# A second stream of small mixers paced against large products: a later start of its turn and a lower rank

## The chip, the cores and the metric

The kernel runs on one core of a Trainium2 chip. The metric is the device time of one execution in microseconds (us). Five engines work side by side, each through its own queue in order: TensorE (PE, with the weight loads as PEld), VectorE (DVE), ScalarE (ACT), GpSimd (POOL) and SyncE (SP), which here only issues transfers.

## What is computed

One trunk layer of a hybrid backbone, for 256 prompt tokens and 2048 latent tokens on a 32 x 64 grid, all in fp32, model width 1024. With `u = h @ w_in` the layer is

```python
u_pool, u_hy, u_q, u_k, u_v = jnp.split(u, [s1, s2, s3, s4], axis=-1)
y_pool = pool_mixer(u_pool, pool_w, pool_scale)          # means over windows 2/4/8/16
y_hy = hyena_mixer(u_hy, ...)                            # two gated long convolutions by FFT
y_na = attend(q, k, v)                                   # q, k after QK-norm
x = x + gate1 * (jnp.concatenate([y_pool, y_hy, y_na], axis=-1) @ w_out)
h = rms_norm(x, norm2_g) * (1.0 + scale2) + shift2
x = x + gate2 * (jnp.square(jax.nn.relu(h @ w_up)) @ w_down)
```

The prompt attends to itself densely; a latent token attends to its grid neighbourhood and to 256 cached keys. The keys and values of the prompt are outputs too. Every large product is made of three fp32r products (high by high, high by low, low by high part), so each weight tile is split in two after it is loaded.

## The kernel before, in words

Three generators write the program; each `yield` gives an abstract cost. `weave` (L177) always takes the next step of the stream with the smallest ratio of cost so far to its weight, so the streams are written down interleaved.

- `dense`, weight 2200e3: first the products for `u` (five blocks of tokens: four of 512 latent tokens, one of 256 prompt tokens), then the q, k and v products (`qkv_run`, `proj_qkv`) for the blocks in the order 3, 4, 0, 1, 2, where 4 is the prompt. I call them qkv3, qkv4, qkv0, qkv1, qkv2. Each but the first begins by loading and normalising its tokens again (`xq`, L164 to L169). Then come output projection and MLP of the prompt and of the four latent bands.
- `latent_mixers`, weight 850e3: the filters of the latent convolutions, then `hyena` (a spectrum stage, an inverse stage, a second of each), then the latent attention, which is written after all q, k, v products and after the prompt's mixers.
- `prompt_mixers` (L856), weight 700e3: waits until qkv4 is written, then writes `prompt_filters` (small fp32 products `pb`), then `prompt_hyena` woven with `pooling` (both for all tokens' pooling and the prompt's convolutions), then the prompt's attention. Its two PSUM banks `b` and `bo` are its own.

The third number of a stream in L1271 is a rank offset. The instructions written in a step of that stream are ranked as if they had been written so many instructions earlier (`tc.high_priority`). When the program is built, a scheduler goes through a simulated run and gives each engine, among the instructions that are ready, the one of the lowest rank; that becomes the order of the engine's queue. The queues are then in order on the chip. Dense has offset 0, the latent mixers 1000, the prompt's mixers 2500.

As the prompt's stream has a ratio of zero when its wait ends, and its whole cost is less than what would bring its ratio level with the other streams, it is written in one piece between qkv4 and qkv0.

Of the kernel before, what the change touches and what calls it, by code (L numbers as in the profile page):

```python
# [55 lines left out]
def tile_hybrid_step(ctx: ExitStack, tc: tile.TileContext, a: dict):  # L56
# [115 lines left out]
    def at_rate(stream, f):  # L172

        for cost in stream:
            yield cost and cost * f

    def weave(*streams):  # L177


        live = [[st[0], float(st[1]), 0.0, st[2] if len(st) > 2 else 0] for st in streams]  # L180
        while live:
            for s in sorted(live, key=lambda e: e[2] / e[1]):
                try:
                    with tc.high_priority(s[3]) if s[3] else ExitStack():
                        cost = next(s[0])
                except StopIteration:
                    live.remove(s)
                    break
                if cost is not None:
                    s[2] += cost  # L190
                    yield cost
                    break
            else:
                yield None
# [10 lines left out]
    def wait_for(*names):  # L205
        while not done.issuperset(names):
            yield None

    def scope(name, bufs=2, side=None, **kw):
        return tc.tile_pool(name=name, bufs=bufs, side=side, reuse_waits="tile", **kw)  # L210
# [644 lines left out]

    def prompt_mixers():  # L856
        yield from wait_for("h2p", "qkv4", "ln")
        with scope("bps", 1, side="right", space=PSUM) as bps:
            def bank(tag="b"):
                return bps.tile([P, 512], F32, tag=tag, name="p" + tag)  # L860

            with scope("pfilt", side="right") as fp:
                yield from prompt_filters(fp, bank)
            with scope("phy", side="right") as fp:
                yield from weave((prompt_hyena(fp, bank), 14000), (pooling(fp, bank), 8100))
            with scope("pat", side="right") as at:
                for hp_ in range(4):
                    yield from attend_prompt(at, bank, hp_)
        done.add("prompt")
# [185 lines left out]
    def latent_mixers():  # L1055
        with scope("aps", 1, space=PSUM) as aps:
            turn = [0]

            def psum(tag=None):
                turn[0] ^= tag is None  # L1060
                return aps.tile([P, 512], F32, tag=tag or "fz"[turn[0]], name="pf")

            yield from filters(psum)
            done.add("filt")
            yield from wait_for("u")
            yield from wait_for("ln")
            with scope("hy") as kp:
                yield from at_rate(hyena(kp, psum), 0.55)
            done.add("hyena")
        yield from wait_for("qkv", "prompt")  # L1070
        with scope("att") as at, scope("attps", 2, space=PSUM) as aps:
            def bank(tag):
                return aps.tile([P, 512], F32, tag=tag, name="p" + tag, bufs={"s": 2, "pt": 2, "o": 1}[tag])

            mask = []
            for rc in range(3):
                for cc_ in range(3):
                    nr, ncol = ROWC[rc][1], COLC[cc_][1]
                    m = at.tile([P, nr, ncol], BF16, tag=f"mask{rc}{cc_}", name="mask", bufs=1)
                    nc.gpsimd.dma_start(out=m, in_=a["mask"][rc * 3 + cc_, :, 0:nr * ncol].rearrange("p (r c) -> p r c", c=ncol))  # L1080
                    mask.append(m)
            for band in range(4):
                yield from wait_for(*(f"qkv{b}" for b in range(max(band - 1, 0), min(band + 2, 4))))
                for hp_ in range(4):
                    yield from attend_latent(at, bank, mask, band, hp_)
                done.add(band)
        done.add("att")
# [180 lines left out]
                        yield from steps  # L1268
                        run = run2

    for cost in weave((dense(ctx.enter_context(ExitStack())), 2200e3), (latent_mixers(), 850e3, 1000), (prompt_mixers(), 700e3, 2500)):  # L1271
        assert cost is not None, "streams wait for each other"


# [175 lines left out]
def build(nc, arrays):  # L1450
    a = {}
    for name, v in arrays.items():
        a[name] = nc.dram_tensor(f"in_{name}", v.shape, mybir.dt.from_np(v.dtype), kind="ExternalInput").ap()
    for name, shape in _OUTS:
        a[name] = nc.dram_tensor(f"out_{name}", shape, F32, kind="ExternalOutput").ap()
    with tile.TileContext(nc, schedule_with_timeline_sim=True) as tc:
        tile_hybrid_step(tc, a)
# [18 lines left out]
```

## Time and profile before

| | us |
|---|---|
| median of 3 runs (lowest to highest) | 3167.44 (3164.95 to 3171.02) |
| the profiled execution | 3163.24 |
| its span, first to last instruction | 3161.5 |
| PE busy | 3022.6 (96%) |
| PEld busy | 2494.6 (79%) |
| DVE busy | 1936.3 (61%) |
| ACT busy | 1428.6 (45%) |
| POOL busy | 951.3 (30%) |

The profiled execution is the source of all rows. A busy PE is not PE at its peak: matmuls overlap and their ends are modelled. PEclk is the granted clock of TensorE as a share of full speed.

### The profile page before, as it was taken

How to read it: one execution, taken by the hardware profiler on the slowest of the kernel's cores; microseconds unless marked ns; L12 is line 12 of the kernel's file. 1: busy time of each engine (PE TensorE's matmuls, PEld its weight loads, DVE VectorE, ACT ScalarE, POOL GpSimd, SP SyncE). 2: the span in 40 equal slices, each digit the busy share in tenths (PEclk: the TensorE clock that was granted, in tenths of full speed). 3: DMA queues.
4: the chain of work that ended last, by engine and by line, in shares of the span. 5: the costliest groups of instructions: out<-in, count | busy, mean ns of one | idle time of the engine just before them, and what ended most of it. 6: DMA issues, size and time to landing. Idle time of an engine off the chain costs nothing.

```text
span 3161.5 us, 46164 instructions
## 1 busy us (share of the span) xinstructions
PE 3022.6 (96%) x16901; PEld 2494.6 (79%) x16901; DVE 1936.3 (61%) x3017; ACT 1428.6 (45%) x2721; POOL 951.3 (30%) x832
## 2 busy tenths in 40 slices
PE   5999998889998999999999999899999999999999
PEld 1667797788988988877878778688878888788887
DVE  7677676987568777876766655544564445634443
ACT  3555445545556666665555543323332333333222
POOL 2333233743243333454433321311231112311101
PEclk8999999999999999999999999999999999999999
DMA  6568667855875865733333325233324233232322
GB/s 222 160 215 298 220 217 244 277 167 169 269 231 184 297 197 161 230 117 107 123 113 119 106 91 189 80 100 107 107 89 152 93 100 114 88 125 94 100 94 87
DMA packets 255167, 494.26 MB, mean 156 GB/s; under 512 B 23763, under 2 KB 124824, under 8 KB 254619
## 3 DMA queue, kind: packets, MB, share of 16 engines
q1 hardware_dynamic: 247741, 469.03, 45.2%
q0 software_dynamic: 7200, 22.28, 2.5%
q8 instruction: 134, 2.20, 0.3%
q14 instruction: 92, 0.75, 0.1%
HBM read 421.86 MB, written 70.13 MB: 156 GB/s over the span
## 4 chain that ended last, share of the span: by engine, by line
PE 81%; DVE 8%; DMA 5%; issue 3%; ACT 2%; POOL 1%; SPq 1%; DVEq 0%; ACTq 0%; POOLq 0%
PE pm L126 22%; PE pm L127 22%; PE pm L128 22%; PE po L923 3%; PE ppt L902 2%; PE ps L888 1%; DVE wl L115 1%; PE ps L889 1%; PE pf L516 1%; PE pf L127 1%; DMA xq<-in_xT_sample 1%; PE pf L126 1%; PE pf L128 1%; PE pf L435 1%; DMA dftw<-in_S 1%
## 5 line engine op out<-in xcount | busy, mean ns | idle before, releaser
L115 DVE TENSOR_TENSOR wl<-wraw,wh 128x1024 fp32r<-128x1024 f32 x460 | 590.3, 1286 | 454.1 <-ACT wh L112 418.9
L112 ACT ACTIVATE wh<-wraw 128x1024 fp32r<-128x1024 f32 x430 | 454.5, 1058 | 781.8 <-PE pm L127 717.6
L126 PE MATMUL pm<-hh,wh 128*128 128x512 f32 (+1 forms) x1920 | 719.3, 377 | 22.7 <-ACT hh L112 12.8
L127 PE MATMUL pm<-hl,wh 128*128 128x512 f32 (+1 forms) x1920 | 718.1, 375 | 1.9 <-DVE hl L166 1.9
L128 PE MATMUL pm<-hh,wl 128*128 128x512 f32 (+1 forms) x1920 | 716.7, 374 | 0.0
L115 POOL TENSOR_TENSOR al<-r,ah 128x512 fp32r<-128x512 f32 (+1 forms) x160 | 200.5, 1255 | 964.6 <-ACT ah L112 959.3
L126 PE MATMUL pm<-ah,wh 128*128 128x512 f32 (+1 forms) x1280 | 473.9, 373 | 7.6 <-ACT r L1132 7.2
L128 PE MATMUL pm<-ah,wl 128*128 128x512 f32 (+1 forms) x1280 | 476.2, 373 | 0.0
L127 PE MATMUL pm<-al,wh 128*128 128x512 f32 (+1 forms) x1280 | 474.1, 371 | 0.0
L126 PEld LDWEIGHTS pm<-hh,wh 128*128 128x128 f32 x1920 | 365.9, 191 | 103.4 <-ACT hh L112 14.2
L127 PEld LDWEIGHTS pm<-hl,wh 128*128 128x128 f32 x1920 | 365.4, 190 | 74.1 <-issue 10.4
L128 PEld LDWEIGHTS pm<-hh,wl 128*128 128x128 f32 x1920 | 365.4, 190 | 69.0 <-issue 7.8
L1150 DVE SCALAR_TENSOR_TENSOR x<-pm,gate,x 128x512 f32<-128x512 f32 (+1 forms) x320 | 220.8, 695 | 286.0 <-PE pm L128 285.0
L126 PEld LDWEIGHTS pm<-ah,wh 128*128 128x128 f32 x1280 | 240.9, 188 | 51.5 <-ACT r L1132 7.4
L127 PEld LDWEIGHTS pm<-al,wh 128*128 128x128 f32 x1280 | 241.3, 189 | 43.1 <-issue 1.9
L128 PEld LDWEIGHTS pm<-ah,wl 128*128 128x128 f32 x1280 | 241.1, 188 | 43.1 <-issue 2.2
L127 PE MATMUL pm<-wl,hh 128*128 128x256 f32 x864 | 250.3, 292 | 5.7 <-DVE wl L115 5.7
L126 PE MATMUL pm<-wh,hh 128*128 128x256 f32 x864 | 248.9, 292 | 6.3 <-ACT hh L165 2.2
L128 PE MATMUL pm<-wh,hl 128*128 128x256 f32 x864 | 250.0, 293 | 2.1 <-POOL hl L115 2.1
L894 POOL TENSOR_SCALAR sS<-sS,rl 128x736 f32<-128x736 f32 (+5 forms) x128 | 125.0, 977 | 197.6 <-DVE rl L893 116.7
L127 PEld LDWEIGHTS pm<-wl,hh 128*128 128x128 f32 x864 | 169.0, 196 | 10.7 <-DVE wl L115 7.1
L126 PEld LDWEIGHTS pm<-wh,hh 128*128 128x128 f32 x864 | 168.0, 196 | 11.7 <-ACT hh L112 3.5
(325 smaller groups left out, 4784.3 us busy)
## 6 DMA issues: line engine op xcount, KB each, us to landing
wraw<-in_w_up SPq DMA_DIRECT2D x160, 512.0 KB
wraw<-in_w_down SPq DMA_DIRECT2D x160, 512.0 KB
wraw<-in_w_qkv SPq DMA_DIRECT2D x60, 512.0 KB
wraw<-in_w_u SPq DMA_DIRECT2D x40, 512.0 KB
dftw<-in_S POOLq DMA_DIRECT2D x40, 512.0 KB, 6.5
wraw<-in_w_out SPq DMA_DIRECT2D x40, 512.0 KB
x<-in_xT_sample SPq DMA_DIRECT2D x64, 256.0 KB
wm<-in_w_mod SPq DMA_DIRECT2D x64, 256.0 KB
```

Source lines behind the costliest of these rows:

```text
L112: nc.scalar.activation(hi, raw, AF.Copy)
L115: lo_eng.tensor_tensor(out=lo, in0=raw, in1=hi.bitcast(F32), op=ALU.subtract)
L126: nc.tensor.matmul(out, lh, rh, start=start, stop=False, **kw)
L127: nc.tensor.matmul(out, lh, rl, start=False, stop=False, **kw)
L128: nc.tensor.matmul(out, ll, rh, start=False, stop=stop, **kw)
L435: nc.tensor.matmul(pf[d][:, e * 256:(e + 1) * 256], lhs(r, e), f3n[r, o * 256:(o + 1) * 256], start=(e == 0), stop=True, skip_group_check= ...
L516: nc.tensor.matmul(pf, f3[r, o * 256 + c * P:o * 256 + (c + 1) * P], h2[r, b * 512:(b + 1) * 512], start=True, stop=True)
L888: nc.tensor.matmul(out, qh[:, qc], krhs, start=True, stop=False, **kw)
L894: nc.gpsimd.tensor_scalar(out=sc_[:, :tot], in0=sc_[:, :tot], scalar1=r, scalar2=1.0, op0=ALU.mult, op1=ALU.mult)
L902: nc.tensor.transpose(tr[:n, q * P:(q + 1) * P], scs[e][:, so:so + n], ident)
L923: nc.tensor.matmul(po[64 * e:64 * e + 64, ocol:ocol + P], vap(e, n), pt[:n, col * P:(col + 1) * P], start=(q == 0), stop=(q == len(chunks) ...
L1150: nc.vector.scalar_tensor_tensor(out=xs[j], in0=po, scalar=gate2[:, j, c:c + 1], in1=xs[j], op0=ALU.mult, op1=ALU.add)
```

## The change

The prompt's stream is charged 80e3 of cost as soon as its wait ends, before it writes anything, and its rank offset goes from 2500 to 1000. No operation is added or removed.

```diff
     def prompt_mixers():
         yield from wait_for("h2p", "qkv4", "ln")
+
+        yield 80e3
         with scope("bps", 1, side="right", space=PSUM) as bps:
...
-    for cost in weave((dense(ctx.enter_context(ExitStack())), 2200e3), (latent_mixers(), 850e3, 1000), (prompt_mixers(), 700e3, 2500)):
+    for cost in weave((dense(ctx.enter_context(ExitStack())), 2200e3), (latent_mixers(), 850e3, 1000), (prompt_mixers(), 700e3, 1000)):
```

## Rows read from the trace of the kernel before

**Rows 1.** Page, first lines: busy us, share of span, instructions.
```profile
PE 3022.6 (96%) x16901; PEld 2494.6 (79%) x16901; DVE 1936.3 (61%) x3017; ACT 1428.6 (45%) x2721; POOL 951.3 (30%) x832
```

**Rows 2.** Windows by engine: start:end, length, busy us and instructions, clock, DMA.
```profile
core 0: us, PE busy (x) PEld busy (x) DVE busy (x) ACT busy (x) POOL busy (x), PEclk, DMA share, GB/s
395.00:495.00 100.00, 99.36 (x685) 90.49 (x685) 68.42 (x82) 43.78 (x84) 32.63 (x27) 1.00 0.64 212
500.00:700.00 200.00, 171.45 (x1121) 149.37 (x1121) 173.71 (x250) 103.46 (x219) 123.11 (x119) 0.91 0.71 233
700.00:900.00 200.00, 186.47 (x1446) 175.79 (x1446) 117.91 (x166) 106.41 (x216) 62.89 (x59) 0.98 0.71 232
```

**Rows 3.** Windows of 50 us, same columns.
```profile
600.00:650.00 50.00, 39.71 (x214) 32.80 (x213) 48.45 (x68) 22.85 (x47) 37.72 (x37) 0.83 0.72 227
...
900.00:950.00 50.00, 50.00 (x424) 50.00 (x423) 41.75 (x60) 28.90 (x55) 19.73 (x15) 1.00 0.65 201
```

**Rows 4.** PE groups at 600:640, then at 680:720: count, busy, mean ns, idle before.
```profile
L126 PE MATMUL pm<-wh,hh 128*128 128x256 f32 x19 | 6.7, 365 | 0.2 <-ACT hh L112 0.2
...
L126 PE MATMUL pm<-wh,hh 128*128 128x256 f32 x92 | 25.7, 284 | 0.0
```

**Rows 5.** By tile: count, ns min/median/max, first and last start.
```profile
L719 SPq DMA_DIRECT2D h2p<-h2pd x1: 562/562/562, 393.4 to 393.4; - x1
...
L850 PE MATMUL pbo<-pS,pw x36: 377/379/796, 529.9 to 682.7; 128*128 128x256 f32 x36
...
L776 PE MATMUL pb<-zp,dpc x32: 377/379/620, 582.0 to 649.8; 128*128 128x256 f32 x32
L796 PEld LDWEIGHTS pb<-Yp,dpc x32: 186/190/338, 608.8 to 680.6; 128*128 128x128 f32 x32
L796 PE MATMUL pb<-Yp,dpc x32: 377/379/797, 608.9 to 680.8; 128*128 128x256 f32 x32
...
L966 SPq DMA_DIRECT2D yTp<-obp x4: 319/398/830, 728.3 to 814.8; - x4
L1104 SPq DMA_DIRECT2D yraw<-yTp x8: 327/332/1458, 875.6 to 979.3; - x8
```

**Rows 6.** DMA issues of SP in order of time: start, length, what is loaded or stored.
```profile
561.56 0.43 SPq L284 DMA_DIRECT2D out_new_kT<-qo  x1
...
605.70 0.82 SPq L1169 DMA_DIRECT2D xq<-in_xT_sample  x2
```

**Rows 7.** DVE groups at 500:700: count, busy us, mean ns, idle before.
```profile
L848 DVE SCALAR_TENSOR_TENSOR pS<-pS,kv,pE 128x256 f32<-128x256 f32 x18 | 13.0, 720 | 2.7 <-POOL pS L836 2.6
...
L847 DVE TENSOR_TENSOR pS<-pS,kv 128x8 f32<-128x8 f32 x4 | 0.6, 154 | 0.0
```

**Rows 8.** DVE groups, then PE groups, at 395:495, same columns.
```profile
L405 DVE RECIPROCAL rinv<-rinv 128x512 f32<-128x512 f32 x2 | 6.7, 3347 | 0.0
...
L747 DVE MEMSET Fp<- 1x256 f32 x2 | 0.5, 272 | 4.3 <-ACT Fp L741 4.3
...
L740 PE MATMUL pb<-kk,dpc 128*128 128x256 f32 x16 | 4.1, 381 | 0.0
...
L750 PE MATMUL pb<-ks,dpc 128*1 128x256 f32 x8 | 2.0, 378 | 0.0
```

**Rows 9.** By line: ns min/median/max of DVE work, and DMA issue by SP.
```profile
L661 DVE TENSOR_TENSOR Y<-Y,Yt x32: 675/684/1792, 550.9 to 1025.9; 128x512 f32<-128x512 f32 x32
...
L115 DVE TENSOR_TENSOR wl<-wraw,wh x460: 1161/1225/2319, 40.6 to 3144.6; 128x1024 fp32r<-128x1024 f32 x154
...
L367 SPq DMA_DIRECT2D dpc<-in_DP x16: 368/403/632, 392.4 to 642.7; - x16
```

**Rows 10.** Who waited on PE, 380:1130: us in total, times, longest.
```profile
PE pm L127 <- DVE wl L115: 5.7, 7, 1.7
```

## The prediction

> **What bounds the kernel now.** I read the page first: PE is busy for 3022.6 of 3161.5 us [rows 1], so work that only changes place is worth nothing unless PE was idle or slow where it stood or where it goes. Then windows, to find where that is. At 395 to 495 PE is busy for 99.4 of 100 us, DVE for 68. At 500 to 700 PE is busy for 171.5 of 200 and DVE for 173.7, and the granted clock is 0.91. At 700 to 900 PE has 186.5, DVE 117.9, clock 0.98 [rows 2]. So one stretch inside the q, k, v products is bound by DVE. Its PE loss is 28.5 us idle plus up to 18 us of missing clock (0.09 of 200): 29 to 47 us, against 13.5 to 17.5 us in the next 200, which also hold two changes of block. The excess is 15 to 29 us.
>
> Then groups and tiles, to see what the stretch holds. At its worst, 600 to 650, DVE is 97% busy, PE makes 214 matmuls where 900 to 950 has 424, and the clock is 0.83 [rows 3]. The dense products all but stop: of one of their three parts, 19 matmuls at 600 to 640 and 92 at 680 to 720 [rows 4]. In that hole qkv0 loads and normalises its tokens (first load at 605.7 [rows 6]), and on DVE and POOL this normalisation stands between the first spectrum of the latent convolution and the prompt's convolution and pooling, whose products run from 529.9 to 682.7 [rows 5]. DVE operations with two SBUF inputs are stretched there: Y, 0.68 us at the median, takes up to 1.79 [rows 9].
>
> **The change, part by part.** Nothing is added or removed; the written place and the rank change.
>
> *Written place.* Costs counted from the code: filters 11.2e3, convolution and pooling ("phase 2") 15.4e3 + 8.1e3 = 23.5e3, attention 12.8e3, in sum 47.5e3. Dense stands at 184.3e3 + 62.4e3 + 31.2e3 = 277.9e3 after qkv4, ratio 0.126; the stream now begins at 80/700 = 0.114 and not at 0. It writes 8.4e3 in one go (most of the filters), then alternates: the last 39.1e3 of its cost take 39.1/700 x 2200 = 123e3 of dense, which is qkv0 and qkv1 (124.8e3).
>
> *Rank.* Counting instructions in the code (an estimate, some 5% loose): qkv3 ranks from 2440, qkv4 from 3940, qkv0 from 4720. The prompt's stream ranks 2280 to 2940 now; after, the filters have 3780 to 4020, phase 2 4090 to 5690, the attention 5690 to 6360. The trace bears the reading out: the stream's first load goes out at 393.4 [rows 5], during qkv3, though it is written after qkv4, whose first result, the prompt's keys, is stored at 561.6 [rows 6]. So the filters move from qkv3 into qkv4, and phase 2, which all ranks ahead of qkv0's normalisation now, will have (4720 - 4090)/1600 = 40% ahead of it and 60% behind, among qkv0's products. The attention (its last store at 814.8 [rows 5]) stays in qkv0 or slides into qkv1.
>
> *A. Filters leave 395 to 495.* PE is the bound there, so their products count: six groups, 4.1 x 3 + 2.3 x 2 + 2.0 = 18.9 us, first and last in [rows 8]. Busy times of pipelined matmuls overlap, so 18.9 is the far end and 0 the other (if the next stretch pays as much). I take -18.9, in the same currency as C.
>
> *B. The DVE-bound stretch.* Phase 2 has thirteen DVE groups at 500 to 700, 48.0 us in sum (first and last in [rows 7]); 60% leaves, -29. The filters arrive: eleven groups, 18.1 us (first and last in [rows 8]). DVE has 11 us less to do where it sets the pace, and the filters' PE work lies in PE's idle time. Ends: 0, if DVE simply takes up spectrum work instead, and -29, the upper excess, if what is out of the way is just what stood ahead of the normalisation. Should the filters arrive and phase 2 not leave, it is +18 (rival 1). I take -11, as it is the balance of rows.
>
> *C. 60% of phase 2's products go to 700 to 900.* (36 + 32 + 32) x 0.379 = 37.9 us [rows 5], 60% is 22.7. PE is idle there for 13.5 us [rows 2]; whatever falls into that is free: +9 to +23. I take +17.7, some 5 us hidden, because idle time there comes in short waits.
>
> *D. DVE in 700 to 900* gets 29 us on top of 118 of 200 [rows 2]: covered by 82 us free. The work that could suffer is the weight split wl, 1.225 us at the median and 2.319 at most [rows 9]; 24 of them in qkv0 and qkv1 make 0 to 26 us of DVE. PE waited for wl only 5.7 us at 380 to 1130 [rows 10]. I take 0, and the far end is a rival.
>
> The Trainium skill, SBUF — State Buffer, "Who interferes with whom", has a rule that speaks against the move: a DVE instruction with two SBUF inputs and a GpSimd instruction that reads SBUF use one shared port, and the one that starts first blocks the other for its whole length. By that rule the stretch of Y above goes along with the pooling to wherever the pooling goes, and the time is that of rival 2; by the medians of the rows alone, D stays at 0.
>
> *Queues moved past.* Phase 2 issues 62 transfers from SP, the filters 19, the attention 28; one takes 0.4 us of SP [rows 9]. 60% of 62 is 37, or 15 us of SP in a stretch of 200: not on the path, 0 to 15, taken 0. POOL's pooling and filter work moves with B. The last consumer: the prompt's output projection loads yTp from 875.6 to 979.3, and the last store is at 814.8 [rows 5]; the attention may slide 60 us before the first load waits. No wait is added; the PSUM banks were the stream's own before and stay so until the same point.
>
> Sum: -18.9 - 11 + 17.7 = -12.2 us. Against the profiled 3163.2 that is 3151; the median of the runs is 4.2 above that execution, so I predict 3155.
>
> **Rivals.**
>
> 1. *No effect.* The scheduler hands PE a ready instruction of any rank when nothing better is ready, so phase 2 keeps its place and only the filters move: A gives -18.9, and 18.1 us of DVE arrive in the bound stretch. -1 us, 3167. For it: phase 2 is a long chain of small steps, and its place is set by its operands as much as by rank. Against it: in the hole DVE has work of all three streams waiting, and there rank decides.
>
> 2. *The hole moves and grows (slower).* Pooling and the prompt's convolution now meet the weight splits of qkv0 and the normalisation of qkv1, and the blocking seen in Y falls on operations that dense waits for directly. The first hole shrinks by B, A and C stand with C in full: -18.9 - 11 + 22.7 = -7; the present excess of 15 to 29 comes again at 700 to 900: +8 to +22, middle +15, so 3182. It decides from the point where PE's idle time at 700 to 900 grows by over 7 us from 13.5. For it: D's far end of 26 us. Against it: no latent spectrum competes for POOL through most of that stretch, POOL being busy for 63 of 200 us against 123 [rows 2].
>
> 3. *The hole closes.* With rank behind qkv0, phase 2 no longer stands ahead of the normalisation, and the stretch becomes as good as the next one: B is -29, A and C cancel to -1. -30 us, 3137. For it: 900 to 950 shows PE without a gap while the second spectrum runs. Against it: the first spectrum keeps its rank ahead of everything, and DVE is then still at 163 of 200 us.
>
> **How the numbers follow.** Forecast 0.45 (own range -26 to 0 us, B and C at their better and worse ends: 3141 to 3167), rival 1 0.20, rival 2 0.20, rival 3 0.15. The range 3136 to 3182 leaves out about half of rival 3 and half of rival 2. A change of 0.2%, 6.3 us, is about what can be told from none, so faster means under 3161.1 and slower over 3173.8. Faster: 0.36 of the forecast, 0.15 of rival 3, 0.03 of rival 1, together 0.54; same: 0.09, 0.14 and 0.02 of rival 2, together 0.25; slower: 0.21, the rest.
>
> **What would show it.** A: the filters' products after 490, the prompt's keys stored before 550. B: DVE's busy time at 500 to 700 (shifted by A) near 163, PE's idle time there near 18, the clock above 0.91, and over 19 dense matmuls in the worst 40 us. C: products of lines 776, 796 and 850 going on past 720. D: wl's median still 1.225 in qkv0. It is wrong if phase 2 still ends before 690, or if the idle time at 700 to 900 grows by as much as it falls before, or if yTp is stored after the projection wants it.

## The result and the profile after

The changed kernel takes 3193.15 us at the median (3188.09 to 3196.84, 4 runs), the kernel before 3167.04 (3164.95 to 3171.02, 4 runs) beside it: ratio 1.0081, 95% interval 1.0067 to 1.0095. It is slower, and outside the predicted range of 3136 to 3182. The profiled execution has a span of 3193.7 us, 32.2 more than before.

The engines' busy times, in the form of [rows 1]:

```profile
PE 3040.5 (95%) x16901; PEld 2507.7 (79%) x16901; DVE 1949.0 (61%) x3017; ACT 1426.5 (45%) x2721; POOL 951.3 (30%) x832
```

The instructions are the same in number. PE is busy 17.9 us longer (3040.5 against 3022.6) with the same work. The mean granted clock of the two executions is 0.978 before and 0.972 after, so about 70 and 89 us of clock are missing: the longer busy time is about what the lower clock accounts for (an estimate from these figures). The other 14.3 us of the span are idle time. The windows of [rows 2] and the first of [rows 3], after the change (busy us and count of PE, PEld, DVE, ACT and POOL, then the mean granted clock):

```profile
core 0: us, PE busy (x) PEld busy (x) DVE busy (x) ACT busy (x) POOL busy (x), PEclk, DMA share, GB/s
395.00:495.00 100.00, 100.00 (x707) 92.25 (x706) 63.95 (x78) 42.69 (x83) 27.64 (x25) 0.99 0.67 210
500.00:700.00 200.00, 167.70 (x1032) 141.65 (x1031) 178.01 (x239) 101.41 (x210) 122.28 (x116) 0.88 0.71 224
700.00:900.00 200.00, 191.07 (x1482) 182.37 (x1482) 132.26 (x204) 113.34 (x235) 67.27 (x66) 0.97 0.76 246
600.00:650.00 50.00, 33.60 (x167) 28.42 (x166) 47.76 (x69) 24.00 (x46) 35.06 (x32) 0.73 0.64 190
```

The stretch that DVE bounds is worse, not better: 1032 matmuls in 500 to 700 against 1121 [rows 2], 167 in its worst 50 us against 214 [rows 3]. 700 to 900 is better. Nearly all the rest was lost in a stretch that the prediction never looked at. Two windows at the end of the convolution, of the kernel before and then of the changed one:

```profile
1000.00:1150.00 150.00, 136.16 (x1062) 130.91 (x1062) 114.72 (x178) 88.22 (x165) 49.95 (x61) 0.92 0.74 245
1050.00:1100.00 50.00, 50.00 (x426) 50.00 (x425) 36.22 (x47) 29.60 (x44) 11.50 (x16) 1.00 0.92 306
```
```profile
1000.00:1150.00 150.00, 123.00 (x926) 113.46 (x924) 98.02 (x188) 86.61 (x191) 53.15 (x64) 0.89 0.73 230
1050.00:1100.00 50.00, 33.49 (x214) 30.86 (x213) 31.27 (x56) 26.37 (x57) 22.97 (x30) 0.76 0.71 202
```

At 1050 to 1100 PE made 426 matmuls without a gap; now it makes 214. Summed by stage (idle time of PE, and the missing clock times the length of the stage, which is the most that the clock can have cost):

| stage (us) | idle before, after | missing clock before, after | difference |
|---|---|---|---|
| 500 to 700 | 28.6, 32.3 | 18, 24 | +3.7 and +6 |
| 700 to 1000 | 17.8, 16.2 | 6, 9 | -1.6 and +3 |
| 1000 to 1150 | 13.8, 27.0 | 12, 16.5 | +13.2 and +4.5 |
| 1150 to 3100 | 27.2, 28.3 | same (0.99) | +1.1 |

Why there: PE's products of the latent convolution (pf) and of the dense stream (pm), each at 500 to 1000 and at 1000 to 1150. First before, then after (busy us and count of PE):

```profile
500.00:1000.00 500.00, 118.13 (x736) 0.95 0.70 227
1000.00:1150.00 150.00, 30.84 (x194) 0.92 0.74 245
...
500.00:1000.00 500.00, 312.77 (x2232) 0.95 0.70 227
1000.00:1150.00 150.00, 106.71 (x804) 0.92 0.74 245
```
```profile
500.00:1000.00 500.00, 131.29 (x817) 0.93 0.69 221
1000.00:1150.00 150.00, 19.30 (x128) 0.89 0.73 230
...
500.00:1000.00 500.00, 292.80 (x2039) 0.93 0.69 221
1000.00:1150.00 150.00, 87.96 (x588) 0.89 0.73 230
```

The convolution is 13.2 us of PE work ahead by 1000, dense 20 us behind. So the convolution's last two stores begin at 1060.7 (before 1092.0) and the prompt's second normalisation, which heads its MLP, starts at 1062.1 (before 1021.7; the matmul of line 154 that sums the squares). The stores after and before, then that matmul before (in brackets: idle us before the instruction, and what ended it):

```profile
L715 SPq DMA_DIRECT2D yT<-yo x2: 327/340/353, 1060.7 to 1061.1; - x2
```
```profile
L715 SPq DMA_DIRECT2D yT<-yo x2: 433/490/548, 1092.0 to 1092.6; - x2
...
1021.67 1.22 PE L154 MATMUL pm<-ssq,ones 128*128 128x256 f32 x2 [0.58 <-POOL ssq L150]
```

Before, the normalisation's work on POOL was over (1036.85) some 50 us ahead of the attention's first mask load (1087.3); now the latent attention opens right inside it. PE's waits there, in the changed kernel:

```profile
1062.14 1.22 PE L154 MATMUL pm<-ssq,ones 128*128 128x256 f32 x2 [2.56 <-POOL ssq L150]
...
1068.22 1.01 PE L126 MATMUL pm<-hh,wh 128*128 128x256 f32 x3 [4.86 <-ACT hh L112]
...
1075.06 0.39 PE L127 MATMUL pm<-hl,wh 128*128 128x256 f32 x1 [2.20 <-POOL hl L115]
...
1080.92 1.01 PE L126 MATMUL pm<-hh,wh 128*128 128x256 f32 x3 [2.77 <-ACT hh L112]
...
1084.55 0.59 PE L890 MATMUL ps<-kst,qh 128*128 128x264 f32 x1 [2.62 <-ACT qh L998]
```

And POOL at the same place, which makes the normalised tokens (xn, hl) in its order of issue; first before, where it takes from 1026.95 to 1036.85, then after:

```profile
1026.95 1.59 POOL L168 TENSOR_TENSOR xn<-x,r 128x256 f32<-128x256 f32 x2 [5.33 <-DVE r L140]
1029.94 1.62 POOL L115 TENSOR_TENSOR hl<-xn,hh 128x256 fp32r<-128x256 f32 x2 [1.40 <-ACT hh L112]
...
1035.15 1.70 POOL L115 TENSOR_TENSOR hl<-xn,hh 128x256 fp32r<-128x256 f32 x2
```
```profile
1065.99 1.59 POOL L168 TENSOR_TENSOR xn<-x,r 128x256 f32<-128x256 f32 x2 [3.90 <-DVE r L140]
1068.25 0.74 POOL L115 TENSOR_TENSOR hl<-xn,hh 128x256 fp32r<-128x256 f32 x1 [0.68 <-ACT hh L112]
1068.93 4.30 POOL L1082 DMA_DIRECT2D mask<-in_mask  x8
1073.72 0.54 POOL L1082 DMA_DIRECT2D mask<-in_mask  x1 [0.49 <-DMA mask<-in_mask]
1074.27 0.74 POOL L115 TENSOR_TENSOR hl<-xn,hh 128x256 fp32r<-128x256 f32 x1
...
1081.92 0.68 POOL L1027 TENSOR_TENSOR Tt<-bias,mask 128x264 f32<-128x264 f32 x1 [6.23 <-issue]
```

The second hl stands behind nine mask loads, 5.3 us, and PE waits for it at 1075.06. In the same microseconds ACT and DVE split the attention's first keys (kst, ckst: ACT 1074.7 to 1078.8, DVE 1075.6 to 1080.0) ahead of the next tokens. That was a reading of the trace; runs e13 to e15 test it. No run separates the mask loads from the splits of keys: of the last three waits above, 7.6 us in sum, only the first, 2.20 us, is for a token that stood behind the mask loads.

### The profile page after: what moved, and what is told of

Its sections match the earlier page's. It is cut to its first block, busy times and chain, and to the rows that moved or that the text cites. A ratio compares the mean times of both kernels' runs of the same rounds, so it can differ in the third digit from the quotient of the medians.

```text
span 3193.7 us, 46135 instructions
## 1 busy us (share of the span) xinstructions
PE 3040.5 (95%) x16901; PEld 2507.7 (79%) x16901; DVE 1949.0 (61%) x3017; ACT 1426.5 (45%) x2721; POOL 951.3 (30%) x832
## 4 chain that ended last, share of the span: by engine, by line
PE 81%; DVE 8%; DMA 5%; issue 3%; ACT 2%; POOL 2%; SPq 1%; DVEq 0%; ACTq 0%; POOLq 0%
PE pm L128 22%; PE pm L126 22%; PE pm L127 22%; PE po L925 3%; PE ppt L904 2%; PE ps L890 1%; PE pf L127 1%; PE ps L891 1%; PE pf L126 1%; PE pf L128 1%; PE pf L435 1%; DVE wl L115 1%; DMA kin<-kT 1%; PE pf L516 1%; DMA yraw<-yT 1%
## 5 line engine op out<-in xcount | busy, mean ns | idle before, releaser
L896 POOL TENSOR_SCALAR sS<-sS,rl 128x736 f32<-128x736 f32 (+5 forms) x128 | 125.0, 977 | 188.3 <-DVE rl L895 97.0
```

Of the source, the lines that this page charges most:

```text
L896: nc.gpsimd.tensor_scalar(out=sc_[:, :tot], in0=sc_[:, :tot], scalar1=r, scalar2=1.0, op0=ALU.mult, op1=ALU.mult)
```

## The experiments

Each kernel differs from the kernel before or the changed one only as its diff says. Ratios are to the kernel before on the same chip, with 95% intervals. Differences between two versions are of their medians; these are from different chips, on which the kernel before took 3165.1 to 3167.0 us, so they are good to some 2 us.

**The two edits apart.** The rank offset of 1000 alone (e1), and the charge of 80e3 alone, which moves the written place (e2).

> The kernel before with the prompt's rank offset 1000 instead of 2500, and no start charge: the stream is still written in one piece between qkv4 and qkv0. Theory 'rank decides' (the lost precedence over the first latent spectrum is what costs): as slow as the changed kernel, 3185 to 3200 us, the second-norm product of the prompt after 1050 us. Theory 'place decides' (the written place is what costs): within 6 us of before, 3161 to 3173.

> The changed kernel with the prompt's rank offset put back to 2500; the start charge of 80e3 stays, so the stream is written alternating with qkv0 and qkv1. Theory 'rank decides': within 6 us of before, 3161 to 3173. Theory 'place decides': as slow as the changed kernel, 3187 to 3199, with the latent convolution ending near 1061 and a PE hole of over 10 us right after it.

e1: 3187.17, ratio 1.0070 [1.0055, 1.0085]. e2: 3182.31, 1.0053 [1.0038, 1.0068]. Either edit alone costs most of the whole, so neither "the rank" nor "the place" is the cause by itself (e2 lies between the ranges of its two theories). Both show what the change shows: the convolution's last stores begin at 1043.5 and 1046.9, the second normalisation stands at 1069.6 and 1048.4, and at 1000 to 1150 PE is busy for 121.1 and 125.0 of 150 us.

**Two theories that fell.** e3 gave the latent mixers a lower rank in the changed kernel, to end the convolution later. e4 gave the normalisation of the tokens of the q, k, v blocks the highest rank, in the kernel before, to close the hole at 600 to 650.

```diff
-(latent_mixers(), 850e3, 1000), (prompt_mixers(), 700e3, 1000))   # e3, on the changed kernel
+(latent_mixers(), 850e3, 300), (prompt_mixers(), 700e3, 1000))
...
             for k in range(KD):                                   # e4, on the kernel before
+              with tc.high_priority(4000):
                 x = xp.tile([P, 512], F32, tag="raw", name="xq", bufs=3)[:, :n]
```

> The changed kernel with the latent stream's rank offset 300 instead of 1000. Theory 'uncovered norm' (the latent convolution now ends as the prompt's second norm begins, so nothing fills PE there): the convolution ends after 1085, PE's idle time in the 50 us after the prompt's output projection falls from 16.5 to under 6, and the time falls by 10 to 20 us, to 3173 to 3183. Rival 'spread loss' (the time goes in many small waits all over the products): the hole may close but the time stays within 6 us of 3193.

> The kernel before with the loading and normalisation of each q, k, v block ranked 4000 instructions earlier, ahead of spectrum and prompt. Theory 'the normalisation queues behind the mixers' work on DVE and POOL in the hole at 600 to 675': the hole shrinks, PE idle at 600 to 700 falls from 17 to under 10, and the time falls by 6 to 15 us, 3152 to 3161. Rival 'the normalisation is held by its buffers (three loads, nine pairs of operands), not by rank': same as before, 3161 to 3173.

e3: 3182.75, 1.0059 [1.0039, 1.0080]. The time lies in the range of its theory, but by luck: the convolution still ended at 1045.2, and PE's idle time at 1050 to 1100 rose from 16.5 to 21.0 us. The lever did not move what it was to move, and the run says nothing on the theory; what it gained shows at 500 to 700, with 1094 matmuls in place of 1032. e4: 3184.32, 1.0058 [1.0043, 1.0074], slower than both of its ranges, and the hole grew: PE idle for 15.8 us at 600 to 650 against 10.3 [rows 3]. The rank of the normalisation is not what makes the hole.

**PE work laid over the normalisation.** The PE instructions of the second inverse stage are queued behind the last products of the prompt's output projection: in the changed kernel (e5), with the charge alone (e6), with the rank alone (e9), and in the kernel before as a control (e7).

```diff
             for i in range(0, 16, 2):
-                z = inverse(hy, 1, i, d1d[1])
+                yield from wait_for(f"step{i // 2}")
+                with tc.issue_after(held[i // 2].ins):
+                    z = inverse(hy, 1, i, d1d[1])
```

(held[0..7] are the last matmuls of steps 13, 14, 15 and five times 16 of the prompt's head.)

> The changed kernel, with the second inverse stage of the latent convolution queued on PE behind the last products of the prompt's output projection, so that it runs during the prompt's second norm as in the kernel before. Theory 'uncovered norm': PE's idle time at 1000 to 1150 falls from 27 to under 16 us and the time by 12 to 20 us, to 3173 to 3181 (the part lost at 500 to 700 stays). Rival 'spread loss': the idle time goes elsewhere and the time stays within 6 us of 3193.

> The start charge alone (offset 2500), with the same queueing of the second inverse stage. Its filters, pooling and convolution run at the times of before, so by 'uncovered norm' nearly all its loss is the hole after the convolution's end: from 3182 down to 3163 to 3173, within 6 us of before. By 'spread loss' it stays at 3178 to 3186.

> The kernel before with the same queueing; there the second inverse stage stands behind the second norm already. By both theories within 6 us of before, 3161 to 3173: it shows that the queueing itself costs and gains nothing.

> The rank half of the change alone (the prompt's mixers at 1000, still written in one lump), with the second inverse stage of the latent convolution queued behind the last products of the prompt's output projection. The half without this took 3187, with PE busy for 121.1 of 150 us at 1000 to 1150 and a granted clock of 0.87 there. Theory, the loss of this half is also the uncovered second normalisation of the prompt: PE at least 130 of 150 us there, the convolution ends behind the second normalisation's products, and 3165 to 3175 in all. Rival, this half loses its time elsewhere (the hole at 500 to 700): PE's busy time at 1000 to 1150 may rise, but 3180 or more.

e7: 3166.94, 1.0008 [0.9998, 1.0017], so the queueing costs nothing by itself. e6: 3170.36, 1.0015 [1.0006, 1.0024], 12 us less than e2. e9: 3173.40, 1.0026 [1.0016, 1.0036], 14 us less than e1. e5: 3185.23, 1.0066 [1.0051, 1.0081], only 8 us less than the change and between its two ranges; PE was idle for 22.7 us at 1000 to 1150, not under 16, of which 8.9 is one wait at 1019 for the residual add of the head, whose tokens arrived late. The place of the loss is confirmed. But these runs also let the convolution end later (1084.3 in e5), so that the mask loads came after the normalisation (in e6 from 1067.9, its last token at 1047.6). Cover and collision move together here.

**What stands in the hole at 500 to 700.** e8: in the kernel before, the pooling is moved behind the prompt's attention.

```diff
-                yield from weave((prompt_hyena(fp, bank), 14000), (pooling(fp, bank), 8100))
+                yield from prompt_hyena(fp, bank)
...
+            with scope("ppool", side="right") as fp:
+                yield from pooling(fp, bank)
         done.add("prompt")
```

(Within the pooling, the prompt's part comes first.)

> The kernel before, with the pooling taken out of the prompt's second phase and put behind the prompt's attention (its prompt pieces first). Theory 'in the hole at 500 to 700 the block change waits for DVE and POOL': 48 us of POOL and 16 us of DVE leave, PE idle at 500 to 700 falls from 28.5 to under 20, and the time falls by 6 to 15 us, to 3152 to 3161, as the latent convolution's end is not moved ahead of the second norm. Rival 'the hole is the latent spectrum's': the hole stays, time 3161 to 3173 or more.

e8: 3172.21, 1.0024 [1.0014, 1.0033]. Its windows at 500 to 700 and at 600 to 650, with the pooling at 773 to 889 (compare [rows 2] and [rows 3]):

```profile
500.00:700.00 200.00, 172.59 (x1167) 152.25 (x1166) 163.09 (x248) 104.44 (x221) 85.17 (x64) 0.92 0.67 217
600.00:650.00 50.00, 34.15 (x193) 27.32 (x192) 46.31 (x71) 24.61 (x47) 25.80 (x18) 0.86 0.69 213
```

At 600 to 650 POOL has a third less to do, DVE is 93% busy all the same, and PE makes 193 matmuls, not more than 214. The hole does not need the pooling. The whole stretch is little changed, with 27.4 us idle against 28.6; the time was lost at 700 to 1000, with 25.5 us idle against 17.8.

**A fourth buffer for the token tiles** (tag "raw", 3 to 4; paid for with one buffer less of ypo, tp and the attention's ptS): in the kernel before (e10), on e5 (e11) and on e6 (e12).

```diff
-                x = xp.tile([P, 512], F32, tag="raw", name="xq", bufs=3)[:, :n]
+                x = xp.tile([P, 512], F32, tag="raw", name="xq", bufs=4)[:, :n]
...
-            pt = at.tile([P, 512], F32, tag="ptS", name="ptS", bufs=5)
+            pt = at.tile([P, 512], F32, tag="ptS", name="ptS", bufs=4)
```

> The kernel before, with four buffers in place of three for the tiles through which a block's normalisation loads its tokens (paid for with one buffer each of the prompt's ypo, tp and the attention's ptS). Theory, the hole at the change into qkv0 is the chain of load, POOL, DVE, ACT and POOL through three buffers: the idle time of PE at 600 to 650 falls from 10.3 us to under 6, and the time by 4 to 10 us. Rival, DVE's load of spectrum and normalisation together sets the hole: 9 us idle or more there, and the time within 4 us of before.

> The changed kernel with the second inverse stage queued behind the prompt's output projection (3185 without more) and four buffers for the token tiles. Theory, what was left of the loss is the chain through three buffers, at the block change (16.6 us idle at 600 to 650) and at the loads of the prompt's head (one wait of 8.9 us at 1019): both fall by half, 3170 to 3177. Rival, the buffers aren't what the waits hang on: 3182 to 3188, with 14 us idle or more at 600 to 650.

> The written place alone, the rank as before, the second inverse stage queued, and four buffers (3170 with three). If the chain through three buffers holds the hole at the block change, 3160 to 3166, below the kernel before; if not, 3168 to 3174.

e10: 3181.99, 1.0051 [1.0038, 1.0063]; e11: 3175.03, 1.0024 [1.0014, 1.0034]; e12: 3179.33, 1.0041 [1.0028, 1.0055]. e10 lost 16 us with 13.8 us idle in the hole, e12 lost 9, both slower than either of their ranges; e11 gained 10, in the range of its theory, but with the 14.4 us idle in the hole that its rival foretold. The buffers do not hold the hole; the gain of e11 is not explained, and the smaller ptS alone may cost part of e10 (PE is 8.9 us less busy at 1150 to 3100 there, in two windows, 784.2 and 1128.6 against 790.3 and 1131.4).

**The attention's opening moved, the convolution left early.** The mask loads on POOL and the first step of the attention on ACT and DVE are queued behind the last operation of the normalisation on each engine: in the changed kernel (e13), with the charge alone (e14), with the rank alone (e15).

```diff
-        yield from wait_for("qkv", "prompt")
+        yield from wait_for("qkv", "prompt", "normed")
...
+                    with tc.issue_after(opened[0]):     # POOL's last hl of the normalisation
-                    nc.gpsimd.dma_start(out=m, in_=a["mask"]...)
+                        nc.gpsimd.dma_start(out=m, in_=a["mask"]...)
...
+                    steps = attend_latent(at, bank, mask, band, hp_)
+                    if band == 0 and hp_ == 0:          # ACT's last hh, DVE's last hl
+                        with tc.issue_after(opened[1]), tc.issue_after(opened[2]):
+                            cost = next(steps)
```

> The changed kernel, with the opening of the latent attention (nine mask loads issued by POOL, the first splits of keys on ACT and DVE) queued on each engine behind the last operation of the prompt's second normalisation; the convolution still ends early. Theory, collision: the uncovered normalisation is also drawn out by that opening, from 8.5 to 16.6 us between its first and last POOL product, so its last POOL product comes within 10 us of its first, PE's idle time at 1050 to 1100 falls from 16.5 to 7 to 10 us, and the time from 3193 to 3181 to 3187. Rival, cover alone: the missing products of the convolution are all there is to it, the chain may be shorter but PE is idle all the same, 13 us or more at 1050 to 1100, 3189 to 3195.

> The written place alone (3182), with the opening of the latent attention queued behind the prompt's second normalisation. Collision: 3171 to 3177, most of what the queued second inverse stage gave (3170). Cover alone: 3179 to 3184.

> The rank alone (3187), with the opening of the latent attention queued behind the prompt's second normalisation. There the mask loads are issued at 1051 to 1057 and the normalisation begins at 1075, so the opening stands ahead of its sums of squares. Collision: 3174 to 3181, with 13 us idle or less at 1050 to 1100 (22.6 without). Cover alone: 3184 to 3190.

e13: 3181.01, 1.0050 [1.0036, 1.0063], 12 us less than the change. e14: 3171.35, 1.0017 [1.0008, 1.0025], 11 less than e2. e15: 3170.53, 1.0020 [1.0010, 1.0029], 17 less than e1 and below both of its ranges. The convolution still ended early (1057.1, 1043.8 and 1044.4). Windows of 1000 to 1150, in the order e1, e2, e13, e14, e15, the changed kernel being above:

```profile
1000.00:1150.00 150.00, 121.12 (x916) 108.45 (x914) 101.34 (x205) 89.12 (x212) 56.13 (x68) 0.87 0.65 210
```
```profile
1000.00:1150.00 150.00, 124.98 (x947) 114.58 (x945) 103.60 (x211) 89.43 (x208) 55.68 (x68) 0.90 0.68 219
```
```profile
1000.00:1150.00 150.00, 131.43 (x1029) 121.94 (x1028) 106.45 (x204) 93.11 (x204) 56.85 (x67) 0.94 0.74 242
```
```profile
1000.00:1150.00 150.00, 130.41 (x1026) 120.31 (x1025) 108.68 (x216) 92.78 (x213) 59.90 (x71) 0.93 0.71 231
```
```profile
1000.00:1150.00 150.00, 132.69 (x1021) 123.56 (x1019) 106.42 (x207) 91.59 (x208) 58.03 (x68) 0.91 0.70 227
```

In e13, e14 and e15 the matmuls come back to 1021 to 1029, of 1062 before. In e13 PE's idle time at 1050 to 1100 fell from 16.5 to 9.0 us, and the normalisation's last POOL operation starts 7.7 us after its first (1062.2 to 1069.9), where the change had 18.9 (1065.99 to 1084.88; the 16.6 us of the expectation go to its last product with r at 1082.56). PE's waits there, in e13:

```profile
1058.63 0.92 PE L156 MATMUL pm<-ssq,ones 128*128 128x256 f32 x2 [2.56 <-POOL ssq L152]
...
1064.40 1.01 PE L128 MATMUL pm<-hh,wh 128*128 128x256 f32 x3 [4.86 <-ACT hh L114]
...
1076.53 0.39 PE L130 MATMUL pm<-hh,wl 128*128 128x256 f32 x1 [0.57 <-DVE wl L117]
```

The first two waits of the changed kernel, 2.56 and 4.86 us, are there as they were: they are the bare normalisation, and nothing covers it. The other three, 2.20, 2.77 and 2.62, are gone: they were the collision, and with them the slow clock (0.90 for 0.76 at 1050 to 1100). One thing moved along: the wait for "normed" also moves the attention's written place. Behind 1150, where nearly all of the attention runs, that gained nothing: PE is idle there (1150 to 3100) for 30.0 us in e13 and 28.3 in the change.

**The latent mixers' rank, with the opening out of the way** (300 in place of 1000): on e13 (e16), on e14 (e17), on the kernel before with the opening queued (e18).

```diff
-(latent_mixers(), 850e3, 1000)
+(latent_mixers(), 850e3, 300)
```

> The changed kernel with the latent mixers at 300 in place of 1000, and the opening of the latent attention queued behind the prompt's second normalisation. With 300 alone it took 3183 and showed 1094 matmuls at 500 to 700 (1032 changed, 1121 before), and its loss stood at 1000 to 1150 (30.5 us idle). Theory: the loss of the change is two things, the hole at 500 to 700 and the attention's opening in the uncovered normalisation, and they add. 3166 to 3173, with 20 us idle or less at 1000 to 1150. Rival: the two give back the same microseconds, 3178 to 3184.

> The written place alone with both levers (latent mixers at 300, opening queued; 3171 with the opening queued alone). Adding: 3162 to 3170. The same microseconds: 3169 to 3174.

> The kernel before with both levers. Its normalisation is covered and ends 50 us ahead of the opening, so queueing does nothing there; the lower rank of the latent mixers lets dense run ahead in the hole at 500 to 700. If the hole hangs on that rank: 3157 to 3164. If not: 3164 to 3172.

e16: 3178.90, 1.0035 [1.0022, 1.0048]: 2 us less than e13, as its rival said. e17: 3188.25, 1.0068 [1.0054, 1.0081], and e18: 3220.45, 1.0174 [1.0160, 1.0188], both outside either expectation. The hole did not shrink (PE idle for 14.0, 17.9 and 21.2 us at 600 to 650), and in e17 and e18 the convolution ended at 1121 and 1196. The rank of the latent mixers is not what opens the hole. Nor is a late end of the convolution a cure: the two kernels in which it ends latest are the slowest of their kind (in e18 PE is idle for 48.8 us at 1150 to 3000, before for 27.2).

## Why the prediction was wrong

**A, the filters leave 395 to 495: right in part.** The prompt's keys are stored at 547.07, before 550 as predicted, 14.5 us earlier than [rows 6]; the term was 18.9. But the other sign, the filters' products after 490, did not come: those on h2p begin at 416.0 (before 397.9), 52 of all 72 still run at 395 to 495, and the last store goes out at 525.4 (before 489.5).

```profile
547.07 0.42 SPq L284 DMA_DIRECT2D out_new_kT<-qo  x1
...
L415 PE MATMUL pb<-f,h2p x8: 376/376/480, 416.0 to 480.3; 64*128 64x256 f32 x8
```

**B failed.** The step priced DVE's time in 500 to 700 as a balance: what leaves, less what arrives. Its own end at 0, "if DVE simply takes up spectrum work instead", is what came, and worse. DVE groups of that stretch after the change, in the form of [rows 7]:

```profile
L661 DVE TENSOR_TENSOR Y<-Y,Yt 128x512 f32<-128x512 f32 x14 | 16.6, 1186 | 0.0
...
L652 DVE TENSOR_TENSOR Y<-pf,F 64x512 f32<-64x512 f32 x15 | 10.2, 677 | 2.0 <-ACT F L646 1.9
...
L848 DVE SCALAR_TENSOR_TENSOR pS<-pS,kv,pE 128x256 f32<-128x256 f32 x16 | 9.1, 572 | 3.2 <-issue 1.7 <-POOL pS L842 1.3
```

The same lines of the kernel before, beside [rows 7]:

```profile
L661 DVE TENSOR_TENSOR Y<-Y,Yt 128x512 f32<-128x512 f32 x12 | 10.7, 894 | 0.0
...
L652 DVE TENSOR_TENSOR Y<-pf,F 64x512 f32<-64x512 f32 x12 | 8.1, 676 | 0.5 <-ACT F L646 0.5
```

The thirteen groups of phase 2 fell from 48.0 to 36.9 us, 23% and not 60%; the spectrum's (lines 652 to 661 and the split ysl) rose from 58.7 to 73.8. DVE went from 173.7 to 178.0 us where 163 was foretold, and PE's idle time from 28.6 to 32.3. Of the filters, 2.4 us came (lines 450, 452, 732, 744, 747 and 751), not 18.1. So what left less what arrived is -8.7, near the -11 of the step; but 15.1 us more of spectrum came on top, and two weight splits fewer were made for dense (18 against 20). PE lost 3.7 us of idle time and up to 6 of clock where B had put -11. The price itself is not borne out either: in e8 DVE is busy for 163.1 us at 500 to 700, just what B foretold, and PE is idle for 27.4, not 18. e8 and e16 to e18 say that neither the pooling nor the latent mixers' rank holds this hole.

The stretching of Y was read in the prediction beside a rule of the Trainium skill, SBUF — State Buffer, "Who interferes with whom", as going along with the pooling. The first half of that reading is not borne out: with the pooling at 773 to 889 (e8), Y still took 1.14 us on the mean at 560 to 690, against 0.90 before (first e8, then before). POOL's splits of the spectrum itself (skl, s2l) run beside it in all of these kernels; the rule does not exclude them, and no run separates them.

```profile
L661 DVE TENSOR_TENSOR Y<-Y,Yt 128x512 f32<-128x512 f32 x12 | 13.6, 1136 | 0.0
```
```profile
L661 DVE TENSOR_TENSOR Y<-Y,Yt 128x512 f32<-128x512 f32 x10 | 8.9, 895 | 0.0
```

**C was over-priced, D was right.** The rank count put 60 of phase 2's 100 products past qkv0's normalisation; 30 of them run past 700 (8, 16 and 6 of the three groups below). The products after, in the form of [rows 5]:

```profile
L776 PE MATMUL pb<-zp,dpc x32: 377/379/484, 649.5 to 706.0; 128*128 128x256 f32 x32
L796 PE MATMUL pb<-Yp,dpc x32: 377/379/483, 668.2 to 723.4; 128*128 128x256 f32 x32
...
L850 PE MATMUL pbo<-pS,pw x36: 377/380/796, 553.3 to 712.9; 128*128 128x256 f32 x36
```

700 to 900 has 36 matmuls more (1482 against 1446 [rows 2]) and yet 4.6 us less idle time (8.9 against 13.5), where the step had foreseen 17.7 us of cost with some 5 hidden. The split wl stayed at 1.225 us at the median, and PE's waits for it in line 127 at 380 to 1130 are 4.4 us (before 5.7 [rows 10]). yTp is stored by 867.1, its first load goes out at 912.7.

**The missing term.** Of the signs of B none came: DVE 178.0 for 163, PE idle 32.3 for 18, the clock 0.88 for above 0.91, and of one part of the dense products 14 in the worst 40 us for over 19. Yet none of the three conditions after "It is wrong if" came true: phase 2 ended at 723, not before 690, the idle time at 700 to 900 fell, yTp was in time. The loss stands at 1000 to 1150, +13.2 us idle and up to 4.5 of clock, over 130 us behind the last store of the stream that was moved (867.1). Rival 2 had the sign and a collision, but another place and other work. What failed is the assumption, made without a row, that only the prompt's stream moves: the sum has no term behind 900, and puts the loss there at nothing without a reason. The instructions are ordered anew over the whole kernel when it is built; the convolution gained 31 us and dense lost 40, and two stages that stood 70 us apart (1021.7 and 1092.0) met.

**Of the 26 us** (3193.15 against 3167.04), the opening's collision is about 11: with the opening moved, 15.4 remain (3181.01 against 3165.59 on its chip, e13). Of these 15, the windows of e13 put 7.6 us of idle time in 500 to 700 (36.2 against 28.6), -3.3 in 700 to 1000, 4.7 in 1000 to 1150 and 2.9 at 1150 to 3100. So less than half of the loss is accounted for by an experiment; the hole at 500 to 700 is located and not explained. Open is why the spectrum runs ahead when the prompt's stream is lowered or written later: the levers tried did not move it. No version ran faster than the kernel before.

One sum of the prediction does not come out: with B and C at their ends, A, B and C add up to -39 to +4 us, and not to the own range of -26 to 0. The result lies outside both.

## What to carry to other kernels

A change of order in a kernel whose instructions are sorted by readiness moves every stream, not only the one that was edited: ask which stream takes the place that comes free, how far ahead it then runs, and what opens when it ends. Look for the chains that only other work covers (a normalisation between two products) and note who covers them now. A stage that opens with DMA issues and splits on the engines of such a chain is better queued behind it: here that gave back 11 to 17 us. Opening it early brought nothing here (PE's idle time at 1150 to 3100 is 27.2 and 28.3 us, whether the first keys are loaded at 1107.7 or at 1070.0).

## What the runs showed of the hardware

A DMA that POOL issues was POOL's own time here: the nine mask loads took 0.535 to 0.593 us each, and the next split began at 1074.27, when the last of them ended (1073.72 + 0.54), though ACT had made its operand hh by 1068.88. On SP the issue of a load took 0.33 us (yTp, [rows 5]) and 0.40 us (dpc, [rows 9]) at the median, and no arithmetic stands behind it, as SP only issues. By the Trainium skill, Perfetto Trace Analysis, "DMA Instruction — SWDGE (GPSIMD)", the profiler's end of such an instruction is when the descriptors have been made, not when the data has moved; the trace agrees, as POOL was free for the split at that moment, while the data of these loads landed 4.3 to 7.3 us after the issue. One of their rows, at 1066 to 1080 (KB each, median us from issue to landing):

```profile
mask<-in_mask POOLq DMA_DIRECT2D x2, 90.0 KB, 6.5
```
